# Two-phase delta-rule heads and attention pairs, with a changed norm, queue and tail, in a hybrid decoder block

## The chip, the cores and the metric

The kernel runs on one core of one Trainium2 chip. The metric is device time in microseconds from the first to the last instruction of one execution, and less is better. The core has five engines with an instruction stream each: TensorE (PE; its weight loads are shown as PEld), VectorE (DVE), ScalarE (ACT), GpSimd (POOL) and SyncE (SP), which here only issues transfers. Each stream runs in the order in which it was laid down when the program was built.

## What is computed

The input x has 2048 rows of 1024 numbers. One layer and a final norm are applied:

```
h = rmsnorm(x)
proj = h @ w_in                       # one wide projection, split among three branches and gate logits
y_a = hgrn2(...)                      # 4 heads, gated linear recurrence
y_b = gated_deltanet(...)             # 4 heads, conv on q,k,v; chunks of 64; T = inverse(I + A)
y_c = sliding_window_attention(...)   # 8 query heads in 4 pairs, window 128, sinks, bias
merged = sum over n of sigmoid(gate_n) * (y_n @ w_branch[n])
out = rmsnorm(x + merged @ w_out)
```

In the delta rule, every chunk needs the inverse of a unit lower triangular 64 x 64 matrix before its state can be advanced, and the state passes from chunk to chunk.

## The kernel before

The 2048 rows are taken in four blocks of 512 (`block`, s = 0 to 3). Large products are made in three passes over a split of each operand into a high and a low part (`mm_ct`, lines 96 to 104, and `mm_tc`, lines 169 to 184): a projection of 128 output channels (`proj_ct`) is 24 matmuls of 128x512 into one of four PSUM banks named "d", a lift of a branch into the model width is 12. Their weights pass through `load_w` (line 78). In the first block they are loaded, split on ACT and DVE and stored; afterwards the split form is loaded ("wHL<-kept", line 83). There are four weight buffers, and all these loads stand in SP's queue.

A block runs: value projections (`proj_v`), four heads of branch A (`unit_a`), four of the delta rule (`unit_b`), four attention pairs (`unit_c`). A `merge(n, yT)` after each branch makes, for each of 8 column tiles, one gate projection (tanh at line 364) and one lift (line 366), and adds them up (lines 370 to 374). The output product (`output`) closes the block. Each unit returns a function that finishes its output (`y_gate`, `y_split`). The small products of the units use two further pairs of PSUM banks, "c0" and "c1", by the parity of the unit.

A delta-rule head h (lines 501 to 667) makes four projections, the convolution (line 514), SiLU, transposes with row sums of squares (lines 521 to 534; the squares are ACT at line 527), the products of line 559, the decay-weighted matrices `NTt` and `QKT` (lines 562, 564), and then inverts. The 16 x 16 diagonal blocks go out to memory in a layout that brings them onto 32 partitions (`scrN`, line 579, read at 582), 28 small DVE instructions invert them (lines 583 to 588), they come back through `scrX` (590, 592), and line 593 transposes them into `X`. Two levels on PE join them (lines 594 to 621, the first matmul of each at line 603, the second at 613), then the products of 630 and 638, and then the scan over four chunks (lines 644 to 662).

An attention pair (lines 680 to 748) makes two projections, and for each half of the block logits (706, 708), a maximum (712), exponentials (720), sums and scaling (728), then transposes of the probabilities (735) and the product with the values (744).

The order of instructions on each engine is worked out when the program is built: a planner follows a priority, which is the order in which the Python code hands the instructions in, takes the first one that its own clock finds ready, and puts later ones ahead where an earlier one is not ready. `tc.issue_after(ins)` holds all instructions of its body that are on the same engine as `ins` behind `ins` in that engine's stream. `last_mm[0]`, `last_act[0]`, `last_ld[0]`, `last_dve[0]` are the last projection matmul, SiLU tanh, weight load and merge product handed in so far. Lines 802 to 834 give the order of units.

For the next block, lines 824 to 829 load x by rows on SP (`load_x`, squares on ACT at line 129), `norm_row` sums, takes the power on POOL, writes the 512 factors to memory and reads them back spread over all partitions (lines 137 and 139). Block 0 has `norm_scale` instead, which spreads the factors by a product of a matrix of ones with diagonals (lines 149, 150).

Of the kernel before, what the change touches and what calls it, by code (L numbers as in the profile page):

```python
# [11 lines left out]
F32 = mybir.dt.float32  # L12
# [8 lines left out]
P = 128  # L21
# [31 lines left out]
def _trunk(tc, S, a, out):  # L53
# [70 lines left out]
    def load_x(s, sq, i, tag="xs"):  # L124
        j, half = i // 2, i % 2
        t = sb.tile([P, TB], F32, name="xs", tag=tag, bufs=2)
        nc.sync.dma_start(t, a["x"][s * TB + j * P:s * TB + (j + 1) * P, half * TB:(half + 1) * TB])
# [3 lines left out]
    rscr = dram.tile([TB], F32, name="rscr", tag="rscr")  # L131

    def norm_row(sq):
# [3 lines left out]
        nc.sync.dma_start(rscr.rearrange("(j p) -> p j", p=P), rs)  # L137
        R = sb.tile([P, TB], F32, name="R", tag="R", bufs=1)
        nc.sync.dma_start(R, rscr.rearrange("(o t) -> o t", o=1).broadcast_to([P, TB]))
        return R  # L140

    def norm_scale(sq):
        rs = sb.tile([P, NT], F32, name="rsx", tag="rsx")
        G.tensor_tensor(rs, sq[:, :, 0], sq[:, :, 1], op=ALU.add)
        rsq(rs, rs, 1.0 / D, EPS)
# [7 lines left out]
        return rs, R  # L153
# [15 lines left out]
    def mm_tc(src, n, lh, ll, step=1, each=None, tags=("d", "d", "d", "d")):  # L169
        pj = [bank(t) for t in tags]  # L170
        for k0 in range(0, KT, step):
# [5 lines left out]
            for j in range(NT):  # L177
                js = slice(j * P, (j + 1) * P)
                for kt in range(k0, k0 + step):
# [3 lines left out]
                    T.matmul(pj[j][:, :n], ll[kt][:, js], wh, start=False, stop=(kt == KT - 1))  # L183
# [5 lines left out]
    def proj_v(s, hH, hL, pj=None, rs=None):  # L189
# [7 lines left out]
        pj = mm_tc(a["wtc"][1], NTC, hH, hL, tags=("d", "d", "c0", "c1"))  # L197
# [20 lines left out]
    rs0, R0 = norm_scale(sq0)  # L218
    v0 = proj_v(0, uH, uL, pj0, rs0)
# [106 lines left out]
    def block(s, hH, hL, last=None):  # L326
# [32 lines left out]
        def merge(n, yT):  # L359
            yH, yL = [[t[:, k, :] for k in range(4)] for t in yT]  # L360
            for dt in range(KT):
                gp = proj_ct(37 + n * KT + dt)
                th = sb.tile([P, TB], F32, name="gth", tag="gth", bufs=GB)
                A.activation(th, gp, AF.Tanh, scale=0.5)  # L364
                lp = bank()
                mm_ct(lp, a["wb"][n, dt], yH, yL, 4)
                if n == 0:
                    m = sb.tile([P, TB], F32, name="msum", tag="msum", bufs=KT + 1)
                    msum.append(m)
                    V.scalar_tensor_tensor(m, th, 1.0, lp, op0=ALU.add, op1=ALU.mult)  # L370
                else:
                    m = msum[dt]
                    last_dve[0] = V.scalar_tensor_tensor(th, th, 1.0, lp, op0=ALU.add, op1=ALU.mult).ins  # L373
                    G.tensor_tensor(m, m, th, op=ALU.add)  # L374
                if n == 2:
                    mH.append(sb.tile([P, TB], F32R, name="mH", tag=SLOT[dt]))
                    mL.append(sb.tile([P, TB], F32R, name="mL", tag="msum", bufs=KT + 1))
                    split(mH[dt], mL[dt], m, 0.5)


# [120 lines left out]
        def unit_b(h):  # L501
# [89 lines left out]
            for r in (0, 64):  # L591
                nc.sync.dma_start(XB[r:r + 64], half(sX, r))
                V.transpose(X[r:r + 64, :, r:r + 64], XB[r:r + 64])
            for lv in (4, 5):
# [4 lines left out]
                if True:  # L599
                    yp = bank(ct)  # L600
                    for c in range(NT):
                        u = (c % 2) * 64
                        T.matmul(yp[u:u + 64, (c // 2) * 64:(c // 2 + 1) * 64], NS[:, c, :], low(X)[:, c],
# [324 lines left out]
```

## Time and profile before

| | us |
|---|---|
| median of three runs | 2512.24 |
| lowest and highest | 2508.59, 2521.8 |
| profiled execution, its own time | 2505.49 |
| its span | 2503.6 |
| PE busy | 2418.3 (97%) |
| DVE / ACT / POOL busy | 1178.4 / 865.7 / 431.1 |

Times in the views are counted from the start of the span. In a timeline, a row has the start, the length, engine, line, operation, output and inputs, shapes and count, and in brackets the idle time of the engine before it and what ended that. The granted clock of TensorE is given as a share of 2.4 GHz.

### The profile page before, as it was taken

How to read it: one execution, taken by the hardware profiler on the slowest of the kernel's cores; microseconds unless marked ns; L12 is line 12 of the kernel's file. 1: busy time of each engine (PE TensorE's matmuls, PEld its weight loads, DVE VectorE, ACT ScalarE, POOL GpSimd, SP SyncE). 2: the span in 40 equal slices, each digit the busy share in tenths (PEclk: the TensorE clock that was granted, in tenths of full speed). 3: DMA queues.
4: the chain of work that ended last, by engine and by line, in shares of the span. 5: the costliest groups of instructions: out<-in, count | busy, mean ns of one | idle time of the engine just before them, and what ended most of it. 6: DMA issues, size and time to landing. Idle time of an engine off the chain costs nothing. (4 is left out here: it accounts for less than half of the span.)

```text
span 2503.6 us, 37412 instructions
## 1 busy us (share of the span) xinstructions
PE 2418.3 (97%) x13634; PEld 1935.1 (77%) x13634; DVE 1178.4 (47%) x3188; ACT 865.7 (35%) x2285; POOL 431.1 (17%) x809
## 2 busy tenths in 40 slices
PE   8999998999999999999999999989999999998998
PEld 7777776778877777677887877768788787876886
DVE  5666575555345535523314553552232454355321
ACT  5454344353324313324223522332322342233221
POOL 3222111211222101111112210111111221111011
PEclk9999998999999999999999999999999999999999
DMA  7756672789944455257774455435666454542555
GB/s 235 255 182 230 219 262 94 230 254 324 306 135 131 147 167 156 87 178 188 247 217 127 138 155 167 140 104 189 175 224 212 125 156 143 163 148 95 169 195 175
DMA packets 195172, 453.63 MB, mean 181 GB/s; under 512 B 53875, under 2 KB 72220, under 8 KB 194860
## 3 DMA queue, kind: packets, MB, share of 16 engines
q1 hardware_dynamic: 194988, 451.24, 56.8%
q8 instruction: 108, 1.77, 0.3%
q14 instruction: 76, 0.62, 0.1%
HBM read 349.60 MB, written 103.14 MB: 181 GB/s over the span
## 5 line engine op out<-in xcount | busy, mean ns | idle before, releaser
L102 PE MATMUL ps_d<-hH,wHL 128*128 128x512 f32 x1952 | 784.6, 402 | 10.8 <-DMA wHL<-kept 8.3
L103 PE MATMUL ps_d<-hL,wHL 128*128 128x512 f32 x1952 | 782.9, 401 | 0.0
L104 PE MATMUL ps_d<-hH,wHL 128*128 128x512 f32 x1952 | 778.7, 399 | 0.7 <-DVE wHL L88 0.7
L102 PEld LDWEIGHTS ps_d<-hH,wHL 128*128 128x128 f32 x1952 | 368.8, 189 | 85.5 <-DMA wHL<-kept 9.4
L104 PEld LDWEIGHTS ps_d<-hH,wHL 128*128 128x128 f32 x1952 | 368.4, 189 | 71.5 <-issue 1.4
L103 PEld LDWEIGHTS ps_d<-hL,wHL 128*128 128x128 f32 x1952 | 368.5, 189 | 68.3 <-issue 2.3
L88 DVE TENSOR_TENSOR wHL<-wraw,wHL 128x512 fp32r<-128x512 f32 (+1 forms) x194 | 131.3, 681 | 96.0 <-ACT wHL L87 92.2
L374 POOL TENSOR_TENSOR msum<-msum,gth 128x512 f32<-128x512 f32 x64 | 89.0, 1397 | 452.9 <-DVE gth L373 442.8
L87 ACT CAST wHL<-wraw 128x512 fp32r<-128x512 f32 (+1 forms) x194 | 113.7, 591 | 126.9 <-PE ps_d L104 82.6
L102 PE MATMUL ps_d<-yH,wHL 128*128 128x512 f32 x384 | 152.9, 402 | 3.4 <-ACT gth L364 2.1
L104 PE MATMUL ps_d<-yH,wHL 128*128 128x512 f32 x384 | 153.6, 400 | 0.0
L103 PE MATMUL ps_d<-yL,wHL 128*128 128x512 f32 x384 | 152.5, 397 | 0.2
L364 ACT ACTIVATE gth<-ps_d 128x512 f32<-128x512 f32 x96 | 57.4, 597 | 270.1 <-PE ps_d L104 267.9
L373 DVE SCALAR_TENSOR_TENSOR gth<-gth,ps_d 128x512 f32<-128x512 f32 x64 | 43.4, 686 | 191.8 <-PE ps_d L104 191.7
L181 PE MATMUL ps_d<-wHL,mH 128*128 128x512 f32 x256 | 99.6, 390 | 1.3 <-DMA wHL<-kept 1.3
L514 DVE SCALAR_TENSOR_TENSOR qkB<-raw,convw,qkB 128x512 f32<-128x512 f32 x96 | 71.6, 746 | 62.1 <-ACT qkB L512 60.8
L182 PE MATMUL ps_d<-wHL,mH 128*128 128x512 f32 x256 | 99.6, 389 | 0.0
L183 PE MATMUL ps_d<-wHL,mL 128*128 128x512 f32 x256 | 99.5, 389 | 0.0
L102 PEld LDWEIGHTS ps_d<-yH,wHL 128*128 128x128 f32 x384 | 71.9, 188 | 19.3 <-ACT gth L364 3.4
L103 PEld LDWEIGHTS ps_d<-yL,wHL 128*128 128x128 f32 x384 | 72.6, 189 | 15.1 <-DVE yL L355 1.7
L104 PEld LDWEIGHTS ps_d<-yH,wHL 128*128 128x128 f32 x384 | 72.8, 190 | 13.8
L414 PEld LDWEIGHTS ps_c<-qk 128*64 128x64 f32 x1536 | 52.5, 137 | 33.3 <-issue 19.6
(282 smaller groups left out, 3747.2 us busy)
## 6 DMA issues: line engine op xcount, KB each, us to landing
wHL<-kept SPq DMA_DIRECT2D x486, 512.0 KB, 3.6
kept<-wHL SPq DMA_DIRECT2D x162, 512.0 KB, 4.2
wraw<-in_wct_dram SPq DMA_DIRECT2D x122, 256.0 KB, 4.0
wHL<-kept SPq DMA_DIRECT2D x32, 324.0 KB, 4.3
xT<-in_xT_dram SPq DMA_DIRECT2D x32, 256.0 KB, 4.2
xs<-in_x_dram SPq DMA_DIRECT2D x32, 256.0 KB, 3.7
rt<-in_x_dram SPq DMA_DIRECT2D x32, 256.0 KB, 4.2
out_dram<-rt SPq DMA_DIRECT2D x32, 256.0 KB, 3.0
```

What stands on the lines that cost most here:

```text
L87: A.copy(w[:, 0, :n], raw[:, :n])
L88: V.tensor_tensor(w[:, 1, :n], raw[:, :n], w[:, 0, :n].bitcast(F32), op=ALU.subtract)
L102: T.matmul(p, wh[:, ks], rh[kt], start=(kt == 0), stop=False)
L103: T.matmul(p, wh[:, ks], rl[kt], start=False, stop=False)
L104: last_mm[0] = T.matmul(p, wl[:, ks], rh[kt], start=False, stop=(kt == nk - 1)).ins
L181: T.matmul(pj[j][:, :n], lh[kt][:, js], wh, start=(kt == 0), stop=False)
L182: T.matmul(pj[j][:, :n], lh[kt][:, js], wl, start=False, stop=False)
L183: T.matmul(pj[j][:, :n], ll[kt][:, js], wh, start=False, stop=(kt == KT - 1))
L364: A.activation(th, gp, AF.Tanh, scale=0.5)
L374: G.tensor_tensor(m, m, th, op=ALU.add)
L414: T.matmul(sp[g * 64:g * 64 + 64, c * 32:(c + 1) * 32], K[:, c * P + g * 64:c * P + g * 64 + 64], qv[:, c, g * nb // 2:(g + 1) * nb // 2, ...
L514: V.scalar_tensor_tensor(dst, raw[:, j:j + TB], convw[:, ti, j:j + 1], dst, op0=ALU.mult, op1=ALU.add)
```

## The change

The second half of a delta-rule head, from the levels at line 594 on, becomes `unit_b2`, and the second half of an attention pair, from the transposes at line 735 on for both halves of the block, becomes `unit_c2`. `unit_b` and `unit_c` return a function that hands in the second half; its first PE instructions are put behind the projection matmul that was handed in last. `merge` is split into `gate` and `lift` and takes a range of column tiles. The norm of the next block uses the product with ones instead of the path through memory. The x loads of that norm, and the `scrN` stores, are issued from ACT's queue. In block 0 the second part of `proj_v` is handed in ahead of `norm_scale`, whose matmuls go behind 8 of its matmul triples. In the last block, the multiplication by `fnorm` of three half rows is joined to the scaling again.

```
-    def load_x(s, sq, i, tag="xs"):
+    def load_x(s, sq, i, tag="xs", eng=nc.sync):
...
-        nc.sync.dma_start(t, a["x"][...])
+        eng.dma_start(t, a["x"][...])
...
-    def norm_scale(sq):
+    def norm_scale(rs, after):
         rp = bank("c0")
         for j in range(NT):
             dg = sb.tile([P, P], F32, name="dg", tag="vn")
             G.tensor_tensor(dg, ident, rs[:, j:j + 1].broadcast_to([P, P]), op=ALU.mult)
-            T.matmul(rp[:, j * P:(j + 1) * P], onesP, dg, start=True, stop=True)
+            with tc.issue_after(after):
+                T.matmul(rp[:, j * P:(j + 1) * P], onesP, dg, start=True, stop=True)
...
-    rs0, R0 = norm_scale(sq0)
-    v0 = proj_v(0, uH, uL, pj0, rs0)
+    rs0 = norm_rows(sq0)
+    marks = []
+    pj1 = mm_tc(a["wtc"][1], NTC, uH, uL, tags=("d", "d", "c1", "c1"), marks=marks)
+    R0 = norm_scale(rs0, marks[2 * NT - 1])
+    v0 = proj_v(0, uH, uL, pj0, rs0, pj1)
...
                 A.copy(NS[r:r + 64], NTt[r:r + 64, :, r:r + 64])
-                nc.sync.dma_start(half(sN, r), NS[r:r + 64])
+                A.dma_start(half(sN, r), NS[r:r + 64])
...
+            return lambda: unit_b2(h, ct, qk, vv, gt, NTt, QKT, KD, LT, XT, X, NS, XB, Y, cols, eq)
+
+        def unit_b2(h, ct, qk, VR, gt, NTt, QKT, KD, LT, XT, X, NS, XB, Y, cols, eq):
+            q, k, VR, d1 = qk[:, 0, :], qk[:, 1, :], b3(VR), cols[:, 0, :]
             for lv in (4, 5):
...
-                    for c in range(NT):
+                    with tc.issue_after(last_mm[0]):
+                        for c in range(NT):
...
+                Es.append((E, cl, b0s))
+            return lambda: unit_c2(j, ct, gt, Es)
+
+        def unit_c2(j, ct, gt, Es):
+            for c2, (E, cl, b0s) in enumerate(Es):
...
-                    for hh in range(2):
-                        for b in range(b0, 2):
-                            T.transpose(...)
+                    with tc.issue_after(last_mm[0]):
+                        for hh in range(2):
+                            for b in range(b0, 2):
+                                T.transpose(...)
...
-                    elif s == NSB - 1 and j < NT - 1:
-                        V.tensor_tensor(t, t, fnorm[:, fs], op=ALU.mult)
...
-                        if half == 0 or (s == NSB - 1 and j < NT - 1):
+                        if half == 0:
...
-        f0 = unit_b(0)
+        pb0 = unit_b(0)
         f3(yA)
-        f1 = unit_b(1)
-        merge(0, yA)
+        pb1 = unit_b(1)
+        f0 = pb0()
+        merge(0, yA, range(2))
+        f1 = pb1()
+        merge(0, yA, range(2, KT))
         yB = new_y()
         f0(yB)
-        f2 = unit_b(2)
+        pb2 = unit_b(2)
         f1(yB)
-        f3 = unit_b(3)
-        f2(yB)
+        pb3 = unit_b(3)
+        pb2()(yB)
         c0 = unit_c(0)
-        f3(yB)
+        pb3()(yB)
         c1 = unit_c(1)
-        merge(1, yB)
+        f0 = c0()
+        merge(1, yB, range(2))
+        f1 = c1()
+        merge(1, yB, range(2, KT))
         yC = new_y()
-        c0(yC)
-        c1(yC)
-        unit_c(2)(yC)
-        unit_c(3)(yC)
+        f0(yC)
+        c2 = unit_c(2)
+        f1(yC)
+        c3 = unit_c(3)
+        c2()(yC)
+        g = [gate(2, dt) for dt in range(3)]
+        c3()(yC)
         if s + 1 < NSB:
             sq = sb.tile([P, NT, 2], F32, name="sqx", tag="sqx")
-            with tc.issue_after(last_ld[0]):
+            with tc.issue_after(last_act[0]):
                 for i in range(2 * NT):
-                    load_x(s + 1, sq, i)
-            R = norm_row(sq)
-        merge(2, yC)
+                    load_x(s + 1, sq, i, eng=A)
+            rs = norm_rows(sq)
+        for dt in range(3):
+            lift(2, dt, g[dt], yC)
+        merge(2, yC, range(3, 6))
+        if s + 1 < NSB:
+            R = norm_scale(rs, last_mm[0])
+        merge(2, yC, range(6, KT))
```

## Rows read from the trace of the kernel before

**Rows 1.** The page: span, TensorE's busy time, its granted clock in 40 slices

```profile
span 2503.6 us, 37412 instructions
...
PE 2418.3 (97%) x13634; PEld 1935.1 (77%) x13634; DVE 1178.4 (47%) x3188; ACT 865.7 (35%) x2285; POOL 431.1 (17%) x809
...
PEclk9999998999999999999999999999999999999999
```

**Rows 2.** Busy time by stretch: stretch, length, PE, PEld, DVE, ACT, POOL busy, PEclk, DMA

```profile
385.00:470.00 85.00, 71.04 (x382) 53.37 (x382) 53.73 (x177) 35.85 (x112) 13.29 (x20) 0.90 0.37 122
1024.00:1071.00 47.00, 39.39 (x216) 28.41 (x215) 25.60 (x82) 14.74 (x48) 7.07 (x12) 0.93 0.25 81
1640.00:1686.00 46.00, 38.57 (x212) 28.05 (x213) 25.11 (x80) 14.43 (x48) 7.07 (x12) 0.93 0.25 81
2257.00:2303.00 46.00, 38.58 (x211) 27.80 (x211) 24.96 (x80) 14.64 (x48) 6.75 (x11) 0.93 0.24 75
```

**Rows 3.** Timeline of PE, 1031 to 1045: levels of the fourth delta-rule head

```profile
1037.58 0.88 PE L603 MATMUL ps_c<-X,NS 128*64 128x64 f32 x8 [0.65 <-DVE X L618]
```

**Rows 4.** Timeline of PE, 986 to 993: small products among large ones

```profile
987.54 0.39 PE L104 MATMUL ps_d<-hH,wHL 128*128 128x512 f32 x1
987.77 0.39 PE L102 MATMUL ps_d<-hH,wHL 128*128 128x512 f32 x1
988.09 0.68 PE L638 MATMUL ps_c<-XB,Y 64*64 64x64 f32 x8
...
991.82 0.27 PE L524 MATMUL ps_c<-ident,qkB 128*128 128x128 f32 x1
```

**Rows 5.** Timeline of ACT, 970 to 1040: the fourth head's first squares, and its NS copies

```profile
1003.78 0.26 ACT L527 ACTIVATE junkB<-ps_c 128x128 bf16<-128x128 f32 x1
...
1009.72 0.83 ACT L578 COPY NS<-NTt 64x256 f32<-64x256 f32 x2 [0.77 <-DVE NTt L562]
```

**Rows 6.** Busy time, columns as in rows 2: levels and scans of the first two heads

```profile
835.00:915.00 80.00, 78.15 (x433) 59.20 (x432) 36.81 (x126) 19.86 (x69) 10.80 (x25) 1.00 0.44 136
```

**Rows 7.** Waits of PE: who waited for whom, us in total, times, longest

```profile
PE ps_c L603 <- DVE X L593: 10.8, 12, 1.8
...
PE ps_d L102 <- DMA wHL<-kept: 8.3, 3, 4.2
```

**Rows 8.** Timeline of SP, 1140 to 1175: the row factors' way through memory

```profile
1148.73 0.46 SPq L83 DMA_DIRECT2D wHL<-kept  x1
1159.24 0.32 SPq L139 DMA_DIRECT2D R<-rscr  x1
```

**Rows 9.** Timeline of PE, 1157 to 1163: the wait for a weight load

```profile
1160.72 0.50 PE L102 MATMUL ps_d<-hH,wHL 128*128 128x512 f32 x1 [2.73 <-DMA wHL<-kept]
```

**Rows 10.** Busy time, columns as in rows 2: after that wait, blocks 1 and 2

```profile
1161.20:1164.60 3.40, 3.40 (x18) 2.62 (x18) 0.00 (x0) 1.07 (x2) 0.00 (x0) 0.51 0.95 245
1775.60:1782.50 6.90, 4.99 (x24) 4.04 (x26) 0.00 (x0) 1.07 (x2) 0.00 (x0) 0.51 0.61 189
```

**Rows 11.** Timeline of all engines, 26 to 50: block 0's norm product

```profile
30.02 1.80 ACT L196 ACTIVATE vA<-ps_d,rsx 128x324 f32<-128x324 f32 x4 [3.22 <-POOL rsx L117]
...
30.52 0.85 PE L150 MATMUL ps_c<-dg,onesP 128*128 128x128 f32 x4 [2.58 <-POOL dg L149]
```

**Rows 12.** Groups by line: x count, then busy us, mean ns, idle before and its ends

```profile
L744 PE MATMUL ps_c<-PT,cv__75 128*64 128x128 f32 x496 | 41.3, 295 | 0.5 <-ACT PT L737 0.3
...
L735 PE MATMUL ps_c<-ident,E 128*128 128x128 f32 x248 | 39.8, 293 | 11.8 <-DVE E L728 11.8
...
L129 ACT ACTIVATE scrp<-xs 128x512 bf16<-128x512 f32 x32 | 20.1, 628 | 13.9 <-DMA xs<-in_x_dram 13.7
```

**Rows 13.** The page's DMA issues: count, KB each, median us to landing

```profile
xs<-in_x_dram SPq DMA_DIRECT2D x32, 256.0 KB, 3.7
```

**Rows 14.** Timeline of DVE, 2488 to 2496: the last block's residual sums and fnorm products

```profile
2494.38 0.69 DVE L768 TENSOR_TENSOR rt<-rt,fnorm 128x512 f32<-128x512 f32 x1 [2.71 <-ACT scrp L764]
2494.99 0.68 DVE L762 TENSOR_TENSOR rt<-ps_d,rt 128x512 f32<-128x512 f32 x1
```

More of the change, by code (lines that the diff above doesn't have):

```diff
@@ L167, in norm_h, with mm_tc @@
         return [hH[:, kt, :] for kt in range(KT)], [hL[:, kt, :] for kt in range(KT)]
-    def mm_tc(src, n, lh, ll, step=1, each=None, tags=("d", "d", "d", "d")):
+    def mm_tc(src, n, lh, ll, step=1, each=None, tags=("d", "d", "d", "d"), marks=None):
         pj = [bank(t) for t in tags]
@@ L182, in mm_tc @@
                     T.matmul(pj[j][:, :n], lh[kt][:, js], wl, start=False, stop=False)
-                    T.matmul(pj[j][:, :n], ll[kt][:, js], wh, start=False, stop=(kt == KT - 1))
+                    last = T.matmul(pj[j][:, :n], ll[kt][:, js], wh, start=False, stop=(kt == KT - 1)).ins
+                    if marks is not None:
+                        marks.append(last)
         return pj
@@ L357, in block, with gate, lift, merge @@
         msum, mH, mL = [], [], []
-        def merge(n, yT):
-            yH, yL = [[t[:, k, :] for k in range(4)] for t in yT]
[L361 to L378, printed above, removed]
+        def gate(n, dt):
+            gp = proj_ct(37 + n * KT + dt)
+            th = sb.tile([P, TB], F32, name="gth", tag="gth", bufs=GB)
+            A.activation(th, gp, AF.Tanh, scale=0.5)
+            return th
+        def lift(n, dt, th, yT):
+            yH, yL = [[t[:, k, :] for k in range(4)] for t in yT]
+            lp = bank()
+            mm_ct(lp, a["wb"][n, dt], yH, yL, 4)
+            if n == 0:
+                m = sb.tile([P, TB], F32, name="msum", tag="msum", bufs=KT + 1)
+                msum.append(m)
+                V.scalar_tensor_tensor(m, th, 1.0, lp, op0=ALU.add, op1=ALU.mult)
+            else:
+                m = msum[dt]
+                last_dve[0] = V.scalar_tensor_tensor(th, th, 1.0, lp, op0=ALU.add, op1=ALU.mult).ins
+                G.tensor_tensor(m, m, th, op=ALU.add)
+            if n == 2:
+                mH.append(sb.tile([P, TB], F32R, name="mH", tag=SLOT[dt]))
+                mL.append(sb.tile([P, TB], F32R, name="mL", tag="msum", bufs=KT + 1))
+                split(mH[dt], mL[dt], m, 0.5)
+        def merge(n, yT, dts):
+            for dt in dts:
+                lift(n, dt, gate(n, dt), yT)
         def unit_a(h):
@@ L600, in unit_b @@
                     yp = bank(ct)
-                    for c in range(NT):
-                        u = (c % 2) * 64
-                        T.matmul(yp[u:u + 64, (c // 2) * 64:(c // 2 + 1) * 64], NS[:, c, :], low(X)[:, c],
-                                 start=True, stop=True, tile_position=(0, u))
+                    with tc.issue_after(last_mm[0]):
+                        for c in range(NT):
+                            u = (c % 2) * 64
+                            T.matmul(yp[u:u + 64, (c // 2) * 64:(c // 2 + 1) * 64], NS[:, c, :], low(X)[:, c],
+                                     start=True, stop=True, tile_position=(0, u))
                     for u in (0, 64):
```

22 lines of the change are left out of this document (8 added, 14 removed).

## The prediction

> **What bounds the kernel.** I read the page first: PE is busy 2418.3 us of 2503.6, so the time is PE's stream and whatever makes it stand or run slowly [rows 1]. A busy share of 97% leaves 85 us. Busy time hides two more losses: stretches in which the granted clock is 1.2 instead of 2.4 GHz, and the small price of changing between large and small products. Next, the list of PE's waits: none is long (1.8 us is the longest behind the triangular solves, 4.2 us behind a weight load), so no single wait decides [rows 7]. Then the waits by place, through busy time by stretch. They sit in one place per block: the end of the fourth delta-rule head. There PE stands 13.96 us in block 0 and 7.61, 7.43 and 7.42 us in blocks 1 to 3, and the clock is granted at 0.90 and 0.93 [rows 2]. Where heads 0 and 1 do the same second half beside plenty of merge work, PE stands 1.85 us in 80 at a full clock [rows 6]. So the same work is nearly free when projections are at hand and dear when they are not.
>
> Why does head 3 end up alone? Its last transposes of q and k start on PE at 991.82 [rows 4], but ACT makes the first square of them only at 1003.78 [rows 5], because in ACT's stream the scan of head 2 stands ahead of it: in the old order head 2's second half is handed in before head 3's first half, and ACT follows the planned order. Head 3's `NS` copies follow at 1009.72 [rows 5], and its last levels run at 1037.58 with nothing between them and a wait before them [rows 3]. By then the two pairs' projections are used up, and the lifts of `merge(1)` lack this head.
>
> **Part 1: delta-rule heads in two phases.** Head 3's first half now goes in ahead of head 2's second half on every engine. Its squares can follow its transposes instead of head 2's scan: 1003.78 - 991.82 = 12 us earlier [rows 4, 5], and with them the solve and `X`. On PE little moves: the old stream already had the next head's four projections ahead of a head's levels, so holding the levels behind `last_mm` costs nothing where they are already there. What changes is that two heads' chains overlap and that the hole has 12 us more of projections, gates and pair work ahead of it. I take the idle time of a hole to fall to what rows 6 show for two second halves with cover, 1.85 us, and in block 0, where ACT and DVE split weights too, to twice that, 3.7 us. That gives (13.96 - 3.7) + (7.61 - 1.85) + (7.43 - 1.85) + (7.42 - 1.85) = 27.2 us. The low clock goes with the idling that precedes it: lost are (1 - clock) x busy time, 0.10 x 71.0 + 0.07 x (39.4 + 38.6 + 38.6) = 15.3 us [rows 2]. Together 42.5 us.
>
> Against this stands the price of cover. A large product takes 987.77 - 987.54 = 0.23 us when a large one follows and 988.09 - 987.77 = 0.32 when a small one does [rows 4]; I take 0.09 for the way back too, so a visit to small work costs 0.18. In the hole some ten groups of small products now run bare (an estimate, from the levels, products and scan steps at lines 603 to 657); with cover each becomes a visit: 4 blocks x 10 x 0.18 = 7.2 us. Part 1 is worth 42.5 - 7.2 = 35.3 us. Bounds: nothing, if the chain is no earlier; 52 us (36.4 idle plus 15.3), if the holes vanish without a price.
>
> **Part 2: attention pairs in two phases.** The transposes of pair 0 go behind pair 1's projections, those of pair 1 behind the first two lifts of `merge(1)`, those of pair 3 behind three gates. The 11.8 us that PE waits for line 728 [rows 12] are the softmax chains that get this cover; most of them lie in the stretches of rows 2 and are counted there, so I add nothing. What is queued behind pair 1's transposes is only the rest of `merge(1)`. If the cover is gone, because a lift waits for head 3, the pair's transposes now wait with it: that is the second rival.
>
> **Part 3: the norm of the next block.** The path through memory held SP: a weight load issued at 1148.73, then the read of the factors, which waits for the write, at 1159.24, so no weight left for 10.5 us [rows 8]. PE then stood 2.73 us for a weight [rows 9]; the longest of the three waits of that kind was 4.2 [rows 7]. Behind these two the clock is 1.2 GHz [rows 10], which costs half the busy time there, 3.40 / 2 + 4.99 / 2 = 4.2 us. Without the path: 2.7 + 4.2 + 4.2 = 11.1 us. The product that replaces it costs eight matmul records, 2 x 0.85 us as in block 0 [rows 11] at most, 1.5 with its visit taken: 3 x 1.5 = 4.5. POOL's four diagonals stand behind the merge sums already handed in, and the last two wait for the first matmuls; only a row factor waits for them, and two merge steps (72 matmuls, 16 us at 0.23) lie behind. Worth 6.6 us; bounds 0 and 11.1.
>
> **Part 4: loads and stores on ACT's queue.** The eight x loads leave SP, and land on ACT, which now issues a load and later waits for it in its own stream. ACT waited 13.7 us for these loads in all, before 32 squares, without PE standing for it [rows 12]. I take 2 us lost; bounds 0 and the third rival. Behind a waiting square stand exponentials, copies of transposes and tanh, and PE needs these for banks. The `scrN` stores on ACT follow their own copies; no row shows a gain on PE, so zero, with the 10.8 us of waiting for `X` [rows 7] as the upper bound.
>
> For moving transfers a page speaks against the change: the Trainium skill, "DMA: Bandwidth & Descriptors", section "Issuing engines are not separate DMA queues", says that transfers from any engine end on the same 16 DMA engines, and that issuing from several saves only the time to initiate. Rows 8 show another cost, SP held 10.5 us by a transfer that waits, which is a matter of the order in a stream; by the page's sentence alone, part 4 would be worth nothing, as it is in the sum.
>
> **Part 5: start and tail.** At the start PE waits for a diagonal until 30.52, but the value projections need a bank that ACT begins to empty only at 30.02 [rows 11]. The wait is therefore replaced by nearly as long a one: 0.5 us, bounds 0 and 2.6. In the tail, DVE's fnorm product at 2494.38 waits 2.71 us for a square and takes 0.69, and the last residual sum stands behind it, at 2494.99 [rows 14]; without it the sum can begin up to 3.4 us sooner, if its matmuls are done by then, and the rest follows. I take 2 us; bounds 0 and 3.4.
>
> **Sum.** 35.3 + 6.6 - 2 + 0.5 + 2 = 42.4 us. The profiled execution took 2505.5 us, so 2463. That execution lies 6.7 us under the median of the three runs, 2512.2; I expect the same distance, and forecast 2470 us for the median.
>
> **Rivals.** First, the hole only moves. Head 3's chain is no earlier, or the earlier chain meets pair 0's exponentials and maxima, now ahead of it on ACT and DVE, and loses the 12 us again. The four stretches keep their idle time, and only parts 3 and 5 count: 2512.2 - 9.1 = 2503 us. For it: the stream is planned before the chip shows real latencies, and 12 waits for `X` say that the plan is early [rows 7]. Against it: the 12 us come from order alone.
>
> Second, the other side: the hole grows. It decides if lifts of `merge(1)` stand in PE's stream ahead of pair 1's second half while head 3 is late. Then the pairs' transposes and value products no longer fill the hole. They are (39.8 + 41.3) / 16 = 5.1 us of PE's time per pair [rows 12]; two pairs in four blocks are 41 us of cover lost on top of the first rival: 2503 + 41 = 2544 us. Against it: the plan puts gates into such a place, as it does now.
>
> Third, ACT is held by its loads. Eight loads per block through two buffers are four rounds of 3.7 us [rows 13], 15 us per block and 44 us in three. About half would reach PE, since four banks of 24 matmuls at 0.23 us cover 22 us: 2470 + 22 = 2492 us. A page bears on it: the Trainium skill, "TensorE: Matmul & The Clock Gate", section "Architectural detail: the array is 16× 32×32, not 1× 128×128", calls ACT and DVE strictly first in, first out. The trace agrees, in the square that waited 12 us behind another head's scan [rows 5].
>
> **How the numbers follow.** Chances: forecast 0.63, first rival 0.17, third 0.11, second 0.09. A change of 0.5%, 12.6 us, is about what a measurement of this kernel can tell from none. The forecast and the third rival are faster, 0.74; the first is the same, 0.17; the second is slower, 0.09. The range reaches down by the better bounds of parts 1 and 3 (17 + 4 us) and some of the solves' waits to 2442, and up past the first rival to 2510. It leaves out the second rival and the outer ends.
>
> **What would show it.** Right: head 3's squares follow its transposes by under 3 us; the stretches around its levels have under 4 us idle and a clock near 1; no row factor passes through memory and PE has no long wait for a weight at a block's end. Wrong: the same idle time at another place, PE waiting in a lift for head 3's output or at line 735, or squares of x on ACT with waits of several us and PE standing for a bank. The prediction falls if small visits among large products rise by far more than 40.

## The result and the profile after

The changed kernel takes 2472.8 us (median; 2470.3 to 2477.8) against 2511.0 for the kernel before beside it: a ratio of 0.984 [0.982, 0.986]. Its profiled execution took 2470.3 us, the one before 2505.5. Single executions of the kernel before and of two of the variants below took 3359 to 3904 us and are left out. The first two rows of its page, which answer to [rows 1]:

```profile
span 2468.6 us, 37448 instructions
...
PE 2403.5 (97%) x13658; PEld 1930.1 (78%) x13658; DVE 1168.6 (47%) x3188; ACT 866.2 (35%) x2285; POOL 437.5 (18%) x821
```

The span is 35.0 us shorter. PE's busy time fell by 14.8 us although it has 24 instructions more, most of it work done at the higher clock, and its idle time by 20.2. By blocks, from the first output matmul of one to that of the next, the four blocks gained 14.5, 3.8, 11.7 and 5.6 us, and what is left lost 0.6. The kernel's lines moved: a delta-rule head's transposes are at L527, its squares at L530, the solve's last step at L596, its levels at L611; an attention pair's transposes at L750, the copies of them at L752, the value products at L759.

The holes first. These are the stretches around the fourth head's levels, with the columns of [rows 2] (stretch, length, busy time of PE, PEld, DVE, ACT and POOL, granted clock, DMA):

```profile
384.00:438.00 54.00, 49.52 (x313) 36.72 (x312) 40.87 (x128) 30.36 (x91) 8.17 (x15) 1.00 0.37 123
1000.00:1048.00 48.00, 46.23 (x296) 35.09 (x298) 32.30 (x111) 23.18 (x73) 5.93 (x12) 1.00 0.30 104
1609.00:1657.00 48.00, 46.25 (x296) 35.12 (x298) 32.29 (x111) 23.18 (x73) 5.91 (x12) 1.00 0.29 99
2216.00:2264.00 48.00, 46.49 (x300) 35.31 (x300) 32.19 (x109) 22.87 (x73) 5.50 (x10) 1.00 0.30 100
```

PE stands 4.48, 1.77, 1.75 and 1.51 us in them, 9.5 in place of 36.4, at a full clock. The first stretch is 54 us long where [rows 2] has 85; from 385 to 470 us the changed kernel stands 4.48 us as well. And the cause that was named: the last transposes of block 1's fourth head on PE, then the first square of it on ACT, then its first levels on PE (start, length, what, idle time before).

```profile
964.64 1.04 PE L527 MATMUL ps_c<-ident,qkB 128*128 128x128 f32 x8
...
1000.86 0.45 PE L611 MATMUL ps_c<-X,NS 128*64 128x64 f32 x8
```

```profile
966.30 0.27 ACT L530 ACTIVATE junkB<-ps_c 128x128 bf16<-128x128 f32 x1
```

The square follows the end of the transposes by 0.6 us, where it stood 12 us behind them before [rows 4, 5], and the levels need no wait. The other blocks agree: from the end of the fourth head's last transpose to its first square it is 11.7 us before, in every block, and 0.5 to 0.9 in the changed kernel.

Now what is late instead. PE's waits (who, for whom, us in total, times, longest):

```profile
PE ps_c L611 <- DVE X L596: 14.7, 9, 2.8
PE ps_c L759 <- ACT PT L752: 7.2, 6, 2.4
...
PE ps_d L102 <- ACT hH L107: 5.6, 1, 5.6
PE ps_c L750 <- DVE E L737: 4.4, 4, 1.7
...
PE ps_d L174 <- DMA wHL<-kept: 3.2, 3, 1.4
PE ps_d L102 <- DMA wHL<-kept: 2.1, 1, 2.1
```

The weight waits at a block's end fell from 8.3 to 2.1 us and those for exponentials from 11.8 to 4.4 [rows 7, 12]. Three grew most: for `X` from 10.8 to 14.7 [rows 7], for the copies of an attention pair's transposes from 0.3 to 7.2 [rows 12], and a wait at the start that was not there. The clock pays for each of them. Busy time by stretch, behind the start's wait, behind a wait for `X` in block 1, behind one for copies, and behind another for `X`:

```profile
43.50:53.70 10.20, 6.49 (x14) 4.63 (x15) 9.06 (x10) 4.92 (x9) 5.49 (x6) 0.50 0.44 167
832.00:835.40 3.40, 3.40 (x9) 2.25 (x10) 1.24 (x6) 1.22 (x4) 0.00 (x0) 0.51 0.16 41
1146.00:1149.40 3.40, 3.37 (x22) 2.85 (x23) 0.43 (x1) 0.72 (x2) 1.69 (x4) 0.50 0.03 11
2047.10:2050.50 3.40, 3.14 (x14) 2.37 (x14) 1.94 (x8) 1.22 (x4) 0.41 (x1) 0.50 0.22 78
```

All four are at the lower of the two levels, 1.2 GHz. The second and the fourth cost half of their busy time, (3.40 + 3.14) / 2 = 3.3 us. PE's timeline at the second:

```profile
831.52 0.45 PE L611 MATMUL ps_c<-X,NS 128*64 128x64 f32 x8 [2.83 <-DVE X L596]
831.91 0.78 PE L102 MATMUL ps_d<-hH,wHL 128*128 128x512 f32 x1
```

**The squares of x on ACT.** ACT's timeline at the end of block 1, then PE's:

```profile
1139.12 0.33 ACTq L127 DMA_DIRECT2D xs<-in_x_dram  x1
1142.73 0.63 ACT L129 ACTIVATE scrp<-xs 128x512 bf16<-128x512 f32 x1 [3.64 <-DMA xs<-in_x_dram]
...
1144.93 0.58 ACT L360 ACTIVATE gth<-ps_d 128x512 f32<-128x512 f32 x1
1145.40 1.06 ACT L752 COPY PT<-ps_c 128x512 f32<-128x512 f32 x2
```

```profile
1142.34 1.03 PE L750 MATMUL ps_c<-ident,E 128*128 128x128 f32 x8
1143.13 0.48 PE L102 MATMUL ps_d<-yH,wHL 128*128 128x512 f32 x1
1146.03 1.97 PE L759 MATMUL ps_c<-PT,cv__74 128*64 128x128 f32 x16 [2.42 <-ACT PT L752]
```

ACT issues a load and then waits 3.64 us for it at the square. The pair's transposes on PE begin at 1142.34, but ACT copies them at 1145.40, behind squares and a tanh, and PE stands 2.42 us. So far this looks like the third rival: ACT held by its loads. In all, ACT waits 25.4 us for x in place of 13.7 [rows 12]. Runs 2, 5 and 12 show below that the queue of the loads is not what made the difference.

**Start.** PE's timeline:

```profile
38.57 0.61 PE L143 MATMUL ps_c<-dg,onesP 128*128 128x128 f32 x4
...
45.90 1.22 PE L102 MATMUL ps_d<-hH,wHL 128*128 128x512 f32 x2 [5.56 <-ACT hH L107]
48.43 0.80 PE L103 MATMUL ps_d<-hL,wHL 128*128 128x512 f32 x1 [1.31 <-DVE hL L108]
```

The norm's product, at 30.52 before [rows 11], now runs at 38.57: behind the whole second projection, not behind 8 of its triples. ACT's `hH` and DVE's `hL`, which are made from the row factors, come later, and PE waits 5.56 + 1.31 = 6.9 us for them. The 500th matmul of the core, counted from 0, starts at 94.96 us; before it started at 91.91.

**Tail.** DVE's last steps:

```profile
2460.73 0.75 DVE L794 SCALAR_TENSOR_TENSOR rt<-rt,ss,fnorm 128x512 f32<-128x512 f32 x1 [1.80 <-POOL ss L117]
2461.40 0.69 DVE L777 TENSOR_TENSOR rt<-ps_d,rt 128x512 f32<-128x512 f32 x1
```

The wait ahead of the last residual sum is still there [rows 14]; it moved from the product with `fnorm` to the scaling of another row, which waits for its factor. From the last matmul's end to the end of the span it is 9.4 us in place of 10.3.

### The profile page after: what moved, and what is told of

It is laid out like the page before. It is cut to its first block, busy times and chain, and to the rows that moved or that the text cites. A ratio compares the mean times of both kernels' runs of the same rounds, so it can differ in the third digit from the quotient of the medians.

```text
span 2468.6 us, 37448 instructions
## 1 busy us (share of the span) xinstructions
PE 2403.5 (97%) x13658; PEld 1930.1 (78%) x13658; DVE 1168.6 (47%) x3188; ACT 866.2 (35%) x2285; POOL 437.5 (18%) x821
## 3 DMA queue, kind: packets, MB, share of 16 engines
q8 instruction: 108, 1.77, 0.3%
## 5 line engine op out<-in xcount | busy, mean ns | idle before, releaser
L102 PE MATMUL ps_d<-hH,wHL 128*128 128x512 f32 x1952 | 785.0, 402 | 7.7 <-ACT hH L107 5.6
L102 PEld LDWEIGHTS ps_d<-hH,wHL 128*128 128x128 f32 x1952 | 369.0, 189 | 76.9 <-ACT hH L107 5.7
L102 PE MATMUL ps_d<-yH,wHL 128*128 128x512 f32 x384 | 153.5, 401 | 0.0
L121 ACT ACTIVATE th<-ps_d 128x512 f32<-128x512 f32 x64 | 38.3, 598 | 130.2 <-PE ps_d L104 120.8
L102 PEld LDWEIGHTS ps_d<-yH,wHL 128*128 128x128 f32 x384 | 72.2, 188 | 14.7 <-issue 0.7
```

Source lines behind the costliest of these rows:

```text
L102: T.matmul(p, wh[:, ks], rh[kt], start=(kt == 0), stop=False)
```

## Experiments

Each ratio stands beside runs of the kernel before on the same chip. Several chips were used, and the kernel before took medians of 2507.5 to 2511.0 us on them, so a difference of 3 us between two medians says little.

**1. The two phases alone**, with start, norm, queues and tail of before.

```
-                A.dma_start(half(sN, r), NS[r:r + 64])
+                nc.sync.dma_start(half(sN, r), NS[r:r + 64])
...
-            with tc.issue_after(last_act[0]):
+            with tc.issue_after(last_ld[0]):
                 for i in range(2 * NT):
-                    load_x(s + 1, sq, i, eng=A)
-            rs = norm_rows(sq)
+                    load_x(s + 1, sq, i)
+            R = norm_row(sq)
...
```

> Only the two phases of heads and pairs, with the start, norm, queues and tail of before. Theory (the gain is the order of the heads): nearly the whole gain, 35 us as in part 1 of the sum, so 2476 us, and the squares of the fourth head still within 3 us of its transposes. Rival (norm, queue and tail carry a good part): 2495 to 2503 us.

Measured: 2491.6 us (2479.0 to 2494.8), 0.992 [0.989, 0.995]. In the profiled execution, which is the fastest of them, the hole is gone:

```profile
996.00:1044.00 48.00, 46.40 (x306) 34.88 (x305) 29.72 (x104) 21.91 (x71) 5.82 (x11) 1.00 0.28 94
```

PE stands 1.6 us there at a full clock, as in the changed kernel. But the waits for `X` and for weights are larger than in either kernel:

```profile
PE ps_c L618 <- DVE X L603: 18.1, 9, 2.8
PE ps_d L102 <- DMA wHL<-kept: 11.5, 3, 5.6
```

So the phases close the holes by themselves, and without the other edits they give part of it back. The time lies between the two expectations: neither held.

**2. The rest alone**: start, norm, queues and tail of the changed kernel, heads and pairs handed in as before.

```
-                nc.sync.dma_start(half(sN, r), NS[r:r + 64])
+                A.dma_start(half(sN, r), NS[r:r + 64])
...
-            with tc.issue_after(last_ld[0]):
+            with tc.issue_after(last_act[0]):
                 for i in range(2 * NT):
-                    load_x(s + 1, sq, i)
-            R = norm_row(sq)
-        merge(2, yC)
+                    load_x(s + 1, sq, i, eng=A)
+            rs = norm_rows(sq)
+        merge(2, yC, range(6))
+        if s + 1 < NSB:
+            R = norm_scale(rs, last_mm[0])
+        merge(2, yC, range(6, KT))
```

> Only the changes of start, norm, queues and tail, units whole as before. The sum of the prediction gives them 7 us: 2504 us, with the stall for a weight at the ends of blocks gone. The trace after speaks for less: the start lost 3 us by the 500th matmul and PE waits for copies behind x loads on ACT; by that 2506 to 2513 us. Rival (they carry the gain): 2480 to 2490 us. The four stretches of idle time at the fourth head should stay.

Measured: 2501.1 us (2494.5 to 2504.8), 0.996 [0.995, 0.998]. The hole stays, 7.27 us idle at a clock of 0.93:

```profile
1027.00:1074.00 47.00, 39.73 (x220) 28.55 (x218) 26.30 (x85) 15.05 (x48) 7.05 (x12) 0.93 0.25 81
```

The holes stay without the phases. On top of the rest the phases are worth 2501.1 - 2472.8 = 28 us; alone they are worth 18. The rest alone is worth 8.5. The difference of 10 us, with an interval of some 8 us either way from run 1 alone, would belong to the two together; run 6 shows where a good part of it can lie. No run changes the norm's path or the tail by itself.

**3 and 4. Heads alone, pairs alone**: run 1 with one of the two parts handed in whole.

```
-        c0 = unit_c(0)
+        c0 = unit_c(0)()
         pb3()(yB)
-        c1 = unit_c(1)
-        f0 = c0()
-        merge(1, yB, range(2))
-        f1 = c1()
-        merge(1, yB, range(2, KT))
+        c1 = unit_c(1)()
+        merge(1, yB, range(KT))
...
```

> Only the delta-rule heads in two phases, pairs whole, all else as before. Theory (the head order frees the end of the fourth head): within 6 us of both phases together, 2476 to 2482 us, and the squares of the fourth head follow its transposes within 3 us. Rival (the pairs' second halves are the cover that counts): 2495 us or more.

```
-        pb0 = unit_b(0)
+        f0 = unit_b(0)()
         f3(yA)
-        pb1 = unit_b(1)
-        f0 = pb0()
-        merge(0, yA, range(2))
-        f1 = pb1()
-        merge(0, yA, range(2, KT))
+        f1 = unit_b(1)()
+        merge(0, yA, range(KT))
...
```

> Only the attention pairs in two phases, heads whole, all else as before. Theory: the fourth head is as late as before, its squares 12 us behind its transposes, the idle stretches stay, so 2508 to 2515 us. The second rival of the prediction prices the cover that the pairs' second halves then no longer give at up to 41 us: 2525 to 2550 us. If pairs alone gain, 2495 us or less, the explanation by the heads is wrong or half.

Measured: heads alone 2470.9, 2483.1 and 2491.1 us, 0.989 [0.984, 0.994], not to be told from run 1; pairs alone 2503.9 us, 0.998 [0.996, 1.000]. With the pairs alone the holes stay:

```profile
1024.00:1071.00 47.00, 41.69 (x250) 30.56 (x248) 24.61 (x78) 16.04 (x50) 7.11 (x12) 0.93 0.27 93
```

With the heads alone PE stands 1.33 us around the same levels, at a full clock:

```profile
1005.00:1053.00 48.00, 46.67 (x309) 35.75 (x308) 31.69 (x108) 21.99 (x72) 5.81 (x11) 1.00 0.32 104
```

The squares go along: 11.7 us behind the fourth head's transposes in blocks 1 to 3 of the rest alone and the pairs alone, 1.5 to 1.8 with the heads or both phases alone. So the gain is the heads' part. Nor is the second rival's price there: pairs in two phases with head 3 still late cost no 41 us.

**5. The x loads back on SP**, all else as changed.

```
-            with tc.issue_after(last_act[0]):
+            with tc.issue_after(last_ld[0]):
                 for i in range(2 * NT):
-                    load_x(s + 1, sq, i, eng=A)
+                    load_x(s + 1, sq, i)
```

> The changed kernel with the x loads of the next block on SP's queue again, all else as changed. Theory (ACT, held by its own x loads, delays the copies at line 752 that PE waits for, 7.2 us with a stretch of low clock): these waits fall under 2 us and the time by 4 to 9 us, 2464 to 2469 us. Rival (SP's queue pays the same in weight loads that come late): 2473 us, with waits of PE for weights of 5 us or more.

Measured: 2464.4 us (2463.7 to 2472.7), 0.982 [0.979, 0.986]: 8.3 us less than the changed kernel by the medians, though the intervals overlap. Of PE's waits:

```profile
PE ps_c L611 <- DVE X L596: 14.0, 9, 2.5
...
PE ps_c L759 <- ACT PT L752: 4.4, 4, 1.7
```

Three of the four executions lie under all of the changed kernel's, one among them. The wait for the copies falls from 7.2 to 4.4 us, not under 2 as the theory had it. The wait for a weight at L102 is not among the ten longest any more, although SP now issues the x loads among the weights; what had held SP was the path through memory, not these loads.

But ACT waits as long for x as before the move. These are ACT's waits for x ahead of its squares and PE's waits for the copies of a pair's transposes, us in total in the profiled execution:

| kernel | pairs | x loads issued by | ACT for x | PE for the copies |
|---|---|---|---|---|
| before | whole | SP | 13.7 | 0.3 |
| run 2, the rest alone | whole | ACT | 13.7 | 0.3 |
| run 3, heads alone | whole | SP | 13.8 | 0.3 |
| run 4, pairs alone | two phases | SP | 21.8 | 4.7 |
| changed | two phases | ACT | 25.4 | 7.2 |
| run 5 | two phases | SP | 25.6 | 4.4 |
| run 11 | two phases | SP | 26.0 | 5.2 |
| run 12 | whole | SP | 14.2 | 0.0 |

Both follow the pairs' phases, not the queue. And the waits for copies over half a microsecond, in all of these kernels, lie in or just behind the stretches in which ACT squares the next block's x, near the ends of the first three blocks; the last block has no next x, and no such wait. By these traces it is the squares, standing in ACT's stream ahead of a pair's copies, that hold PE once the pairs are in two phases. How much of the 8.3 us is the queue's is not shown.

**6. The `scrN` stores back on SP**, all else as changed.

```
-                A.dma_start(half(sN, r), NS[r:r + 64])
+                nc.sync.dma_start(half(sN, r), NS[r:r + 64])
```

> The changed kernel with the stores of the 16 x 16 blocks on SP's queue again. The prediction gives this move zero, with up to 11 us as the other end: 2473 us if zero. Rival (on SP the store stands behind weight loads that wait for a buffer, so the solve ends later and PE's wait at line 611 grows): 2476 to 2484 us, with that wait above 17 us in place of 14.7.

Measured: 2485.4 us (2473.7 to 2494.1), 0.991 [0.987, 0.994]: 12.6 us more, and outside the changed kernel's interval.

```profile
PE ps_c L611 <- DVE X L596: 19.4, 10, 2.8
```

The prediction had put this edit at zero, and the rival came, a little above its range, though one of its five executions, at 2473.7 us, lies within the changed kernel's range. The price is clock for the most part. Against the profiled execution of the changed kernel, the one here, which is the slowest of the five, has 18.9 us more of busy time for the same matmuls (2422.4 against 2403.5) and 4.8 us more of idle time. This is one such stretch, behind a wait of 2.63 us for `X` at 2204.61:

```profile
2206.10:2226.60 20.50, 20.50 (x74) 12.93 (x73) 6.63 (x28) 2.19 (x7) 0.00 (x0) 0.50 0.21 60
```

Why the waits for `X` grow is only half shown. The store itself goes out as early on either queue, 0.43 us behind the start of the `NS` copy; but on SP it holds the queue for 36.2 us in all, until the copies are made, with the weight loads and reads behind it. At the even heads, where PE waits, `X` is ready 0.5 us later in blocks 1 to 3 (32.9 instead of 32.4 us behind the head's last transposes, means), and PE's waits there grow by 3.3 us in all. At the odd heads it is ready 3.4 us later, and PE waits no longer there. The same stores stood on SP in run 1, with waits of a similar size; this is what the phases and the rest can have in common in run 2.

The Trainium skill, "DMA: Bandwidth & Descriptors", section "Issuing engines are not separate DMA queues", says that starting transfers on several engines saves only the time to start them; by that sentence alone neither move should matter. For the stores the runs differ, by 12.6 us clear of noise; the 8.3 us of the loads are not clear of it.

**7 and 8. The start**: the norm's product handed in in the middle of the second projection; and the start of before.

```
-    pj1 = mm_tc(a["wtc"][1], NTC, uH, uL, tags=("d", "d", "c1", "c1"), marks=marks)
-    R0 = norm_scale(rs0, marks[2 * NT - 1])
+    spread = []
+    def middle(kt):
+        if kt == 2:
+            spread.append(norm_scale(rs0, marks[2 * NT - 1]))
+    pj1 = mm_tc(a["wtc"][1], NTC, uH, uL, each=middle, tags=("d", "d", "c1", "c1"), marks=marks)
+    R0 = spread[0]
```

> The changed kernel with block 0's norm product handed in after two of the eight steps of the second value projection, instead of after all. Theory (the product now stands behind the whole projection, so that PE waits 5.6 us for the first normed tiles and runs on at a low clock): the wait shrinks to 2 us or less, the 500th matmul moves from 95 to 87 us, and the time falls by 5 to 8 us, 2465 to 2468 us. Rival (the normed tiles take 13 us of DVE and ACT work whatever comes first, and the wait only moves): 2472 us.

```
-    pj1 = mm_tc(a["wtc"][1], NTC, uH, uL, tags=("d", "d", "c1", "c1"), marks=marks)
-    R0 = norm_scale(rs0, marks[2 * NT - 1])
-    v0 = proj_v(0, uH, uL, pj0, rs0, pj1)
+    R0 = norm_scale(rs0, None)
+    v0 = proj_v(0, uH, uL, pj0, rs0)
```

> The changed kernel with the start of before: block 0's norm product ahead of the second value projection. Theory (the new start costs 3 us, read at the 500th matmul, 95.0 against 91.9 us): that matmul back at 91.9 to 92.5 us and the time 3 to 6 us less, 2467 to 2470 us. Rival (what is lost at the start is caught up later, because a later wait ends at a fixed time): 2472 to 2474 us.

Measured: 2476.0 us, 0.986 [0.983, 0.988], with the product in the middle. The theory missed. The wait has only changed its name:

```profile
PE ps_d L104 <- DVE wHL L88: 3.4, 1, 3.4
```

and PE waits 1.9 us for the diagonals besides. The 500th matmul starts at 94.56, not at 87. With the start of before: 2468.7 us, 0.985 [0.982, 0.987], and the 500th matmul at 91.12. By the ratios neither differs from the changed kernel; the place in the trace does, by 3.8 us, and there the old start is better.

**9. Gates as cover.** One gate of `merge` is handed in ahead of the second half of heads 0 and 2.

```
         pb1 = unit_b(1)
+        ga = gate(0, 0)
         f0 = pb0()
-        merge(0, yA, range(2))
+        lift(0, 0, ga, yA)
+        merge(0, yA, range(1, 2))
...
         pb3 = unit_b(3)
+        gb = gate(1, 0)
         pb2()(yB)
...
-        merge(1, yB, range(2))
+        lift(1, 0, gb, yB)
+        merge(1, yB, range(1, 2))
```

> The changed kernel with one gate of the merge handed in ahead of the second half of heads 0 and 2, which puts 12 more large matmuls, 2.8 us, ahead of the first level of these heads. Theory (even heads now wait longer for X because the next head's first half stands ahead of their solve on DVE, 32 us instead of 28): the wait at line 611, 14.7 us, falls under 5 us and the time by 6 to 12 us with the clock, 2461 to 2467 us. Rival (the chain of the even head sets the later work, so that the wait appears elsewhere): 2471 to 2475 us.

Measured: 2459.7 us (2458.8 to 2463.2), 0.980 [0.977, 0.982]: 13 us less than the changed kernel, with no execution in common, and a little more than the theory had.

```profile
PE ps_c L611 <- DVE QKT L567: 4.9, 6, 1.5
...
PE ps_c L611 <- DVE X L596: 2.6, 5, 0.9
```

The waits at L611 go from 14.7 to 7.5 us in all, not under 5, but none is over 1.5, and the low clock behind them goes too. There are now 17 instead of 5 large matmuls between the next head's last small products and the first level, in blocks 1 to 3. So the long waits of the even heads go when PE has more to do ahead of them.

**10. All mends together**: gates, x loads on SP, the start of run 7, and in the tail the last sum handed to DVE ahead of the third scaling.

```
+                            with tc.issue_after(added[0]) if s == NSB - 1 and j > 1 else ExitStack():
-                            V.scalar_tensor_tensor(t, t, ss, fnorm[:, fs], op0=ALU.mult, op1=ALU.mult)
+                                V.scalar_tensor_tensor(t, t, ss, fnorm[:, fs], op0=ALU.mult, op1=ALU.mult)
```

> The changed kernel with x loads on SP, the start's product in the middle, the gate ahead of even heads, and in the tail the last residual sum ahead of the third scaling. If the causes are separate, the gains add: 5 + 6 + 8 + 2, so 2450 to 2458 us. If they are shares of one thing, 2462 us or more.

Measured: 2457.0 us (2454.9 to 2459.4), 0.978 [0.976, 0.981], inside the range for separate causes. Singly the edits gave 13, 8.3 and, for the start, -3.2 us, 18 in all, and together 16, with the tail's edit, which was not run singly; whether they add exactly these runs can't tell.

**11. The same with the start of before.**

```
-    pj1 = mm_tc(a["wtc"][1], NTC, uH, uL, each=middle, tags=("d", "d", "c1", "c1"), marks=marks)
-    R0 = spread[0]
-    v0 = proj_v(0, uH, uL, pj0, rs0, pj1)
+    R0 = norm_scale(rs0, None)
+    v0 = proj_v(0, uH, uL, pj0, rs0)
```

> The changed kernel with the gate ahead of even heads, x loads on SP, the start of before and the tail with the last residual sum ahead of the third scaling. Theory (start, x loads, cover and tail are separate losses): 3 us under the run with all four edits that had the product in the middle, 2450 to 2455 us. Rival (the start is caught up): 2457 us.

Measured: 2453.7 us (2451.4 to 2457.6), 0.979 [0.977, 0.981]. That is the theory's time, but the 3 us between this run and run 10 are within the noise. In the tail 8.6 us are left behind the last matmul. Among PE's longest waits is still one for the copies of a pair's transposes, although SP issues the x loads. PE's timeline, then ACT's:

```profile
1133.18 1.03 PE L748 MATMUL ps_c<-ident,E 128*128 128x128 f32 x8
...
1134.51 0.40 PE L104 MATMUL ps_d<-yH,wHL 128*128 128x512 f32 x1
1136.97 1.15 PE L757 MATMUL ps_c<-PT,cv__74 128*64 128x128 f32 x16 [2.06 <-ACT PT L750]
```

```profile
1135.23 0.63 ACT L129 ACTIVATE scrp<-xs 128x512 bf16<-128x512 f32 x1 [1.34 <-DMA xs<-in_x_dram]
...
1136.34 1.06 ACT L750 COPY PT<-ps_c 128x512 f32<-128x512 f32 x2
```

ACT stands for x, squares it, makes a tanh, and only then copies the transposes that PE had finished 2 us before.

**12. Run 11 with the attention pairs whole.** This asks whether the pairs' phases themselves cost something.

```
-        c0 = unit_c(0)
+        f0 = unit_c(0)()
         pb3()(yB)
-        c1 = unit_c(1)
-        f0 = c0()
+        f1 = unit_c(1)()
         lift(1, 0, gb, yB)
-        merge(1, yB, range(1, 2))
-        f1 = c1()
-        merge(1, yB, range(2, KT))
+        merge(1, yB, range(1, KT))
...
-        g = [gate(2, dt) for dt in range(3)]
-        c3()(yC)
+        unit_c(3)()(yC)
...
```

> The best version so far (gate ahead of even heads, x loads on SP, start of before, changed tail; 2453.7 us) with the attention pairs whole again. Theory (the heads carry the change, the pairs' second halves add what stands at line 735 in before, at most 11.8 us with low clock): 2456 to 2466 us, with PE's waits at the transposes of the pairs back to 8 us or more. Rival (the pairs in two phases add nothing): 2452 to 2456 us. Second rival (they cost cover): under 2450 us.

Measured: 2445.9 us (2444.0 to 2448.3), 0.974 [0.972, 0.976]: the fastest of all, 7.8 us under run 11 and 27 under the changed kernel. The second rival held, and the theory was wrong by 10 us. PE's timeline at the place of the fences of run 11, then ACT's copies:

```profile
1120.34 1.23 PE L747 MATMUL ps_c<-ident,E 128*128 128x128 f32 x8
1121.33 0.48 PE L104 MATMUL ps_d<-hH,wHL 128*128 128x512 f32 x1
...
1122.43 1.09 PE L756 MATMUL ps_c<-PT,cv__74 128*64 128x128 f32 x16
```

```profile
1121.46 1.05 ACT L749 COPY PT<-ps_c 128x512 f32<-128x512 f32 x2
```

Between a pair's transposes and its value products there are four large matmuls, and PE doesn't wait. In run 11 there were three and in the changed kernel one, so cover alone is not the difference: the copies begin 1.1 us behind the start of the transposes here, and 3.2 us in run 11, where a square of x stands ahead of them. In all, ACT waits 14.2 us for x in place of 26.0, and PE not at all for the copies (table in run 5). By blocks, counted as above, run 12 gains 4.7 and 3.1 us on run 11 in blocks 1 and 2 and 0.8 in the last, which has no next x; block 0 gains 0.3. So in this setting pairs are better whole, and ACT's stream is the place to look; that a missing gate is what costs was not shown. Pairs alone (run 4) came out 5.7 us under the kernel before, at the edge of noise; no gain of that kind is seen here.

**Not run.** Laid out without the two `issue_after` holds of the second halves, the streams of all five engines are the same. Those holds bind nothing here; the order in which the halves are handed in does it all.

## Why the prediction was right, and where not

The forecast was 2470 us, with 2442 to 2510 around it; the time is 2472.8. The mechanism and the largest term hold. That the number comes so close is luck in part: some smaller terms are wrong by more than that distance, and cancel. The sum gave 42 us between profiled executions and 35 came; and the 6.7 us that were added on the way from the profiled execution to the median are 2.4 in the changed kernel.

**Part 1, right in cause and size.** Idle time of the four stretches: forecast 27.2 us less, found 36.4 - 9.5 = 26.9. Low clock in them: 15.3, all regained. The signs that it named came, but for block 0, whose stretch has 4.48 us idle where under 4 were expected. The 12 us of the squares came from the order on ACT. Not all of them reach `X`: in blocks 1 to 3 the `NS` copy of the fourth head starts 10 us earlier behind its last transposes, its `X` is ready 6.6 us earlier (34.0 in place of 40.6), because the solve shares DVE with more work now. No run holds the cover and moves the chain alone, so the shares of the earlier chain and of the work put ahead of the levels are not told apart. Changes between large and small products rose by 36 in the four blocks; at 0.09 us that is 3.2 us, where 7.2 were forecast: fewer groups of small products ran bare than the ten estimated.

**Not in part 1: the even heads.** The step that failed is that holding the levels "costs nothing". It looked at PE's stream alone. For heads 0 and 2 in blocks 1 to 3 (means), PE reaches the first level 3.1 us later behind the head's last transposes than before, but `X` is ready 4.2 us later, 32.4 in place of 28.2 us. On DVE, too, the next head's first half now stands among this head's solve, whose steps take 10.7 us in place of 7.9. In all PE waits 14.7 - 10.8 = 3.9 us more for `X` and loses 3.3 to the clock: 7.2 us. That DVE's order is the cause is read from its stream; run 9 shows only that cover on PE takes the long waits away.

**Part 2, "I add nothing" wrong in both directions.** The waits for exponentials fell by 7.4 us, part of them in the holes. But the waits for the copies came with the pairs' phases, as the table in run 5 shows: 6.9 us more, and 1.7 for the low clock at 1146. The prediction asked what stands behind a pair's transposes on PE, and not what stands ahead of their copies on ACT. In run 12, without the pairs' phases, these waits are gone and the kernel is 7.8 us faster.

**Part 3, its gain right.** Forecast 11.1 us for waits and low clock, found 8.3 - 2.1 = 6.2 of waits and the 4.2 of clock [rows 10], which is at full level there now. This is read from the trace, and no run takes the path through memory back alone. What the new product costs was not measured by itself.

**Part 4, both terms mis-sized, in opposite directions.** The x loads cost 8.3 us by the medians of run 5 where 2 were taken; the intervals leave room for less. The third rival asked for 22 us through ACT's queue. Its mechanism, PE standing because ACT stands for x, is in ACT's timeline: the copy at 1145.40 came behind a square that had waited 3.64 us. The Trainium skill, "TensorE: Matmul & The Clock Gate", section "Architectural detail: the array is 16× 32×32, not 1× 128×128", which calls ACT strictly first in, first out, agrees with it. But ACT stands as long when SP issues the loads, 25.6 us against 25.4; so the rival had the engine right and the reason wrong. The `scrN` stores, put at zero with 10.8 us as the upper bound, are worth 12.6 by run 6, most of it clock. The bound was PE's waits for `X` before, and counted no clock. Where the prediction calls part 4 worth nothing, "as it is in the sum", its sum has -2 us for the loads.

**Part 5, wrong in sign.** Start: 0.5 us gained was forecast, 3.1 were lost by the 500th matmul. The step that failed took "behind 8 matmul triples" as the place of the norm's product; it is the earliest place, and the product came behind all. Runs 7 and 8 show that the middle is no better. Tail: 2 us forecast; 0.9 came between the last matmul and the end, and waits for weights in the last output took 1.4. The fnorm product was rightly seen as late, but the scaling that now stands ahead of the last sum waits too, 1.80 us for its row factor.

**The balance.** 26.9 + 15.3 - 3.2 - 7.2 + 10.4 - 8.6 - 3.1 - 0.5 = 30 us of the 35; the 8.6 are the 6.9 by which the wait for the copies grew and half of the low clock at 1146, which parts 2 and 4 share. The stores are in no term of it. Some 5 us are in many small waits, those for exponentials outside the holes among them, and were not placed one by one.

**The rivals.** The first fell with the four stretches, the second with run 4, and the third came true in what PE waits for, at less than half its price, and not in the cause.

## What to carry to other kernels

A hole in the bound engine that follows from the order on another engine closes when the halves of the work are handed in so that each chain starts at once; but every half moved ahead changes what stands ahead of the next consumer on every engine, so it is counted place by place: PE's cover for `X` at the even heads, ACT's squares ahead of a pair's copies. Moving a transfer to another queue is to be tried and timed: 12.6 us came with the stores on ACT, while the loads moved there gained nothing and the waits in front of their squares were the same on either queue. A hold is the earliest place of an instruction, not its place.

## What the runs showed of the hardware

The price of a short wait was not expected to vary so much. In the changed kernel the granted clock fell to 1.2 GHz for 3.4 us behind waits for `X` of 2.83 and 2.35 us, and not behind one of 2.38. In the profiled execution of run 6, six waits of 2.4 to 2.8 us in blocks 1 to 3 were followed by 0, 3.4 (three times), 13.7 and 20.5 us at the low level. In the heads alone there is such a stretch too:

```profile
2201.90:2222.30 20.40, 20.40 (x73) 12.81 (x73) 6.54 (x27) 2.09 (x7) 0.00 (x0) 0.50 0.21 60
```

PE is busy for all of it: the low clock stayed though nothing was waited for, and cost 10 us for a wait of under 3. What decides was not found.

Executions of one kernel differ with it. Run 6 ranges over 20 us, from a granted clock of 0.984 to 0.995. Runs 1 and 3, which like run 6 have the heads in two phases and the stores on SP, range over 16 and 20 us, runs 9, 11 and 12 over 4 to 6. But that short waits make a kernel unsteady is not shown: the changed kernel ranges over 7 us and run 8, with waits for `X` of up to 2.8 us, over 2, in four executions each.
